# A hybrid decoder block on one core: the forms of the output products land in their places, two sets in turn on ScalarE's queue, with a third weight buffer and loads issued behind weight loads

## The chip, the cores and the metric

The program runs on one core of a Trainium2 chip. A core has TensorE (PE, matmuls), VectorE (DVE), ScalarE (ACT), GpSimd (POOL) and SyncE (SP), which work through instruction lists of their own and wait for one another by semaphores, and 16 DMA engines that move data between the chip's memory and the core's own memory. A transfer is issued by an instruction on one engine's list and then runs by itself; the engine waits at that instruction until what the transfer needs is there. The metric is device time in microseconds of one execution, the median of several runs; lower is better.

## The reference, cut to what matters

One decoder layer over 1024 tokens and 16 meta tokens, width 1024: half a SwiGLU step, a mixing step (a gated DeltaNet beside RWKV-7), half a SwiGLU step, a norm. The change lies in the two SwiGLU steps, and there in the second product.

```python
def _swiglu(x, w_gu, w_down):
    gate, up = jnp.split(x @ w_gu, 2, axis=-1)
    return (jax.nn.silu(gate) * up) @ w_down

h = h + 0.5 * _swiglu(_rmsnorm(h, ffn1_norm[l]), ffn1_w_gu[l], ffn1_w_down[l])
u = _rmsnorm(h, mix_norm[l])
...
h = h + merged @ w_out[l]
h = h + 0.5 * _swiglu(_rmsnorm(h, ffn2_norm[l]), ffn2_w_gu[l], ffn2_w_down[l])
return _rmsnorm(h, final_norm)[:, N_META:]
```

All of it is float32; w_gu is 1024 x 5632 and w_down 2816 x 1024.

## The kernel before, in words

**Precision.** A float32 matmul is made of three in the reduced type fp32r: `split` (lines 164 and 165) writes the high part of a tile on ScalarE (a copy, rounded) and the low part on VectorE (source minus high part); then high x high, high x low and low x high are added up in one accumulator. Every weight and every operand passes through such a pair of instructions.

**The two SwiGLU steps.** Each is a "gate_up" stage and a "down" stage, named gate_up1 and down1 for the first, gate_up2 and down2 for the second. Both stages use a product of 2 x 2 blocks by seven block products instead of eight. For down, tokens are cut into halves (columns of the transposed activations, n = 520 in the first step, 512 in the second) and the 2816 inner rows into two halves of 11 tiles of 128. The seven operands made of the activations' blocks are called **forms** (`FORMS`: b11, t1, t2, b22, t3, b21, t4); each has 11 tiles of 128 x n float32, 260 or 256 KB a tile. gate_up makes them unit by unit and stores them to memory (`frm`), on SP's list. In its last unit b11 is formed first, and t4 last.

**down** (from line 647) has seven rounds, r0 to r6, one for each form. A round runs over four m (128 output rows), and over two weight chunks of each m, of 6 and 5 inner tiles (128 x 768 and 128 x 640, 384 and 320 KB). For each chunk it multiplies 6 or 5 tiles, 3 times, for both column halves of n (in ffn2, n = 512 is one piece). So a round of down1 has 264 matmuls (line 667), one of down2 132 of twice the width. After each m the sum is added to up to four residual tiles (`h`, `hh`, line 673, VectorE): 4 of them in r0, then 2, 3, 1, 2, 1, 1. In down1 the rounds r5 and r6 are run twice, for columns 256 on and for the first 256, so that the norm of the next step can begin early; there each weight chunk is fetched twice and used for half as many matmuls.

**Weights.** `fetchw` takes a raw tile (`wraw`, two buffers), loads it on SP's list (line 233), splits it into a tile `w` (two buffers) and keeps one chunk ahead of the use (`AHEAD` = 1). In r0, r5 and r6 the raw tile is split itself. In r1 to r4 the weight is a sum or difference of blocks: POOL adds or subtracts the raw tile and a standing tile `wsum` (lines 239 to 246), and r1 and r4 load a second block into `wsum` first (lines 238, 245).

**Forms before.** `Hidden.load` loads a form tile into one of three staging tiles `hr` on SP's list (line 623). `Hidden.fill` splits it into a slot of a ring of 28 (tiles `fa`, `fb` in ffn1; `hdb`, `fs` in ffn2), as many tiles ahead of the round as slots allow. The residual tiles are loaded on POOL's list, all at the head of down (lines 735 and 834).

**What sets the order.** The builder emits instructions through a scheduling layer, so an engine's list is not the order of the code; the rows quoted with the change are from the built programs. Each engine's list is worked in order.

Of the kernel before, what the change touches and what calls it, by code (L numbers as in the profile page):

```python
# [227 lines left out]
def down_weights(g, name, raw, r, m, k0, kk):  # L228
# [4 lines left out]
    dma(raw, blk(*((0, 0), (1, 1), (0, 0), (0, 1), (1, 0), (0, 1), (1, 1))[r]))  # L233
    if r in (0, LAST, LAST + 1):
        return raw
    s = g.wsum[:, m, k0 : k0 + kk]
    if r == 1:
        dma(s, blk(1, 0))
        sums(s, s, raw, op=ALU.add)
    elif r == 2:  # L240
        sums(s, s, raw, op=ALU.subtract)
    elif r == 3:
        sums(s, raw, s, op=ALU.subtract)
    else:
        dma(s, blk(0, 0))
        sums(s, s, raw, op=ALU.subtract)
# [3 lines left out]
def fetchw(g):  # L250
# [10 lines left out]
    w = g.wp.tile([P, 2, KD, P], F32R, name="w", tag="w", bufs=WB)  # L261
# [4 lines left out]
def loadw(g, name, *idx):  # L266

    while g.wfetched < min(g.wused + 1 + AHEAD, len(g.worder)) and g.worder[g.wfetched]:
# [341 lines left out]
class Hidden:  # L610

    AHEAD = 3

    def __init__(self, g, pool, n):
        self.g, self.pool, self.n, self.raws, self.loaded = g, pool, n, [], 0
        self.order = [(r, p) for r in range(len(FORMS)) for p in range(HF)]
        self.slots, self.at = [], {}

    def load(self):
        r, p = self.order[self.loaded]  # L620
        self.loaded += 1
        raw = self.pool.tile([P, ROW(self.n)], F32, name="hr", tag="hr", bufs=self.AHEAD)[:, : self.n]
        self.g.nc.sync.dma_start(raw, self.g.frm[r, p][:, : self.n])
        self.raws.append(raw)

    def ahead(self):
        for _ in range(self.AHEAD):
            self.load()
        yield
        yield  # L630
        fetchw(self.g)
        yield
        yield
# [12 lines left out]


def slot_tile(pool, n, name):
    return pool.tile([P, 2, ROW(n)], F32R, name=name, tag=name, bufs=1)[:, :, :n]


def down(g, hs, which, n, hidden, hooks):

    nc = g.nc
    hidden.fill(HF + 5)
    for r, cols in down_rounds(which == 1):
        hidden.fill(HF * (r + 1))
        for m in range(HK):
            pd = mm_tile(g, "pd", n)
# [15 lines left out]
            if r <= LAST:  # L675
                hidden.fill(HF * r + 16 + 3 * (m + 1))
# [1143 lines left out]
```

## Time and profile before

| | us |
|---|---|
| median of 3 runs | 3102.53 (3102.46 to 3102.97) |
| the profiled execution | 3106.87 |
| its span, first to last instruction | 3105.1 |
| gate_up1's last products to the end of down1's matmuls | 468.65 to about 770 |
| gate_up2's last unit to the end of down2's matmuls | about 2811 to 3090 |
| TensorE busy over the span | 2928.2 (94%) |
| VectorE, ScalarE, POOL busy | 2192.1 (71%), 1456.7 (47%), 493.1 (16%) |
| mean granted TensorE clock | 0.981 |

The page's chain of waits gives the share of the span by the engine and line that the end waited for. The windows view gives, for each stretch of time, the busy time of every engine with its instructions in brackets, then the granted clock, the DMA engines' busy share and the rate in GB/s. A timeline row is a start, a length, engine, line and operation, and in square brackets the idle time before it and what ended that. Busy shares of the whole span say little here: down1 and down2 are some 18% of it and have limits of their own. A few matmul records can be missing, so counts differ by some from 264.

### The profile page before, as it was taken

What the parts mean: (1) busy time and instruction counts of PE and PEld (TensorE: products, weight loads), DVE (VectorE), ACT (ScalarE), POOL (GpSimd) and SP (SyncE); (2) the same over time, 40 slices, a digit from 0 to 9 for tenths busy, and PEclk for the clock granted to TensorE, in tenths of its full rate; (3) what the DMA queues carried; (4) which work ended last, traced back from release to release, by engine and by line L of the source; (5) the groups of instructions that cost most, each with busy time, mean ns of one, the idle gap of its engine ahead of it and who ended that gap; (6) DMA issues with size and microseconds to landing.
All of it is one profiled execution on the core that took longest, in us unless ns stands there. A gap on an engine that the chain in (4) does not pass through costs nothing.

```text
span 3105.1 us, 63103 instructions
## 1 busy us (share of the span) xinstructions
PE 2928.2 (94%) x25630; PEld 2519.8 (81%) x25630; DVE 2192.1 (71%) x4103; ACT 1456.7 (47%) x2562; POOL 493.1 (16%) x574
## 2 busy tenths in 40 slices
PE   8999997998989999999998999999999999998897
PEld 8999997887978888888776777777786888886676
DVE  7566666755677777877877888777766766666874
ACT  5222223334655565665566556665644432223343
POOL 0333321511010000000000100000000032331520
PEclk9999998999999999999999999999999999999999
DMA  3333237656223223332332332223345233336753
GB/s 124 98 103 103 103 132 243 211 149 174 90 66 77 62 70 82 79 84 73 100 93 71 78 83 79 77 73 84 109 146 177 75 106 102 102 102 224 237 174 111
DMA packets 294467, 351.52 MB, mean 113 GB/s; under 512 B 173392, under 2 KB 179536, under 8 KB 294176
## 3 DMA queue, kind: packets, MB, share of 16 engines
q1 hardware_dynamic: 289936, 335.68, 36.1%
q0 software_dynamic: 2512, 8.65, 0.8%
q8 instruction: 201, 3.29, 0.5%
q10 hardware_dynamic: 1728, 3.16, 0.3%
q14 instruction: 90, 0.74, 0.1%
HBM read 279.50 MB, written 67.91 MB: 112 GB/s over the span
## 4 chain that ended last, share of the span: by engine, by line
PE 66%; DVE 15%; DMA 8%; ACT 7%; issue 3%; SPq 0%; POOL 0%; DVEq 0%; ACTq 0%; POOLq 0%
PE pg L486 24%; PE pp L299 18%; PE pd L667 5%; DMA hr<-frm 4%; DVE w L165 3%; PE pg L510 3%; PE pwo L299 3%; ACT w L164 2%; DMA wraw<-in_wdn 2%; DVE tb L1482 1%; DVE Xb L1484 1%; PE vp L1167 1%; PE cs L1114 1%; PE mp L1167 1%; PE bkt L1399 1%
## 5 line engine op out<-in xcount | busy, mean ns | idle before, releaser
L299 PE MATMUL pp<-uk,w 128*128 128x512 f32 (+2 forms) x4824 | 969.3, 346 | 11.1 <-DVE w L165 6.0
L299 PEld LDWEIGHTS pp<-uk,w 128*128 128x128 f32 x4824 | 743.1, 190 | 107.9 <-DVE w L165 13.4
L165 DVE TENSOR_TENSOR w<-wraw,w 128x1024 fp32r<-128x1024 f32 (+2 forms) x314 | 393.8, 1255 | 112.4 <-ACT w L164 105.2
L164 ACT ACTIVATE w<-wraw 128x1024 fp32r<-128x1024 f32 (+2 forms) x314 | 314.4, 1002 | 284.6 <-PE pg L486 130.4
L486 PE MATMUL pg<-bt,w 128*128 128x256 f32 (+2 forms) x2520 | 404.2, 319 | 7.4 <-ACT w L164 6.7
L486 PEld LDWEIGHTS pg<-bt,w 128*128 128x128 f32 x2520 | 362.1, 189 | 42.2 <-ACT w L164 7.2
L492 DVE TENSOR_TENSOR c<-c,pg 128x520 f32<-128x520 f32 (+1 forms) x280 | 189.5, 689 | 245.8 <-PE pg L486 222.4
L486 PE MATMUL pg<-b,w 128*128 128x256 f32 (+2 forms) x2160 | 347.8, 317 | 0.0
L486 PEld LDWEIGHTS pg<-b,w 128*128 128x128 f32 x2160 | 309.7, 188 | 28.1
L667 PE MATMUL pd<-fa,w 128*128 128x256 f32 (+1 forms) x1200 | 173.5, 299 | 40.5 <-DVE w L165 19.1
L667 PEld LDWEIGHTS pd<-fa,w 128*128 128x128 f32 x1200 | 159.7, 201 | 51.1 <-DVE w L165 24.7
L164 ACT ACTIVATE w<-wrx 128x1024 fp32r<-128x1024 f32 (+1 forms) x64 | 58.4, 912 | 290.9 <-PE pg L486 247.7
L667 PE MATMUL pd<-fs,w 128*128 128x512 f32 x636 | 155.8, 401 | 14.0 <-ACT w L164 7.6
L456 POOL TENSOR_TENSOR wrx<-wrx 128x512 f32<-128x512 f32 x38 | 52.9, 1392 | 726.2 <-DVE w22b L165 547.2
L667 PEld LDWEIGHTS pd<-fs,w 128*128 128x128 f32 x636 | 122.0, 194 | 45.4 <-ACT w L164 9.8
L1484 DVE TENSOR_TENSOR Xb<-Xb,tb 115x126 f32<-115x126 f32 (+22 forms) x496 | 125.3, 253 | 8.8
L1482 DVE TENSOR_TENSOR tb<-Ub,Xb 115x126 f32<-115x126 f32 (+22 forms) x496 | 124.0, 250 | 8.3 <-DMA Ub<-scr 1.0
L1291 DVE SCALAR_TENSOR_TENSOR acc<-xr,pk,acc 128x528 f32<-128x528 f32 (+1 forms) x144 | 108.7, 756 | 29.1 <-ACT acc L1287 28.2
L299 PE MATMUL pwo<-uk,w 128*128 128x512 f32 x384 | 99.9, 413 | 4.1 <-DVE w L165 1.9
L165 DVE TENSOR_TENSOR w<-wsum,w 128x768 fp32r<-128x768 f32 x64 | 75.0, 1173 | 24.5 <-ACT w L164 24.1
L299 PEld LDWEIGHTS pwo<-uk,w 128*128 128x128 f32 x384 | 73.9, 197 | 21.9 <-ACT w L164 2.6
L164 ACT ACTIVATE w<-wsum 128x768 fp32r<-128x768 f32 x64 | 50.2, 785 | 83.5 <-PE pd L667 67.0
(441 smaller groups left out, 4940.4 us busy)
## 6 DMA issues: line engine op xcount, KB each, us to landing
wraw<-in_win SPq DMA_DIRECT2D x150, 512.0 KB
wraw<-in_wdn SPq DMA_DIRECT2D x64, 384.0 KB
wraw<-in_wgu SPq DMA_DIRECT2D x44, 512.0 KB
wrx<-in_wgu SPq DMA_DIRECT2D x44, 512.0 KB
wraw<-in_wdn SPq DMA_DIRECT2D x64, 320.0 KB
frm<-c SPq DMA_DIRECT2D x77, 260.0 KB
hr<-frm SPq DMA_DIRECT2D x77, 260.0 KB
frm<-c SPq DMA_DIRECT2D x77, 256.0 KB
```

The source lines that it names most:

```text
L164: g.nc.scalar.activation(hi, src, AF.Copy)
L165: (eng or g.nc.vector).tensor_tensor(lo, src, hi.bitcast(F32), op=ALU.subtract)
L299: g.nc.tensor.matmul(ps, lhsT=l, rhs=r, start=i == 0, stop=i == n - 1)
L456: sums.tensor_tensor(a22, a21, a22, op=ALU.add)
L486: nc.tensor.matmul(ps[:, c0 : c0 + cn], lhsT=l[:, x, k, :], rhs=r[:, k, y, c0 : c0 + cn], start=i == 0, stop=i == 3 * HK - 1)
L492: nc.vector.tensor_tensor(o, x, y, op=ALU.add)
L510: nc.tensor.matmul(ps[:, c0 : c0 + cn], lhsT=l[:, x, k, :], rhs=r[:, k, y, c0 : c0 + cn], start=i == 0, stop=i == 6 * HK - 1)
L667: nc.tensor.matmul(pd[:, c0 : c0 + cn], lhsT=wd[:, u, k - k0, :], rhs=x[:, v, c0 : c0 + cn], start=k + i == 0, stop=k == HF - 1 and i == 2)
L1167: g.nc.tensor.matmul(ps[e][HS[dst], c0 : c0 + CB], lhsT=l, rhs=r, start=True, stop=True)
L1291: nc.vector.scalar_tensor_tensor(acc[:, :n], xr[:, tap : tap + n], V("convw", ct * 4 + tap), acc[:, :n], op0=ALU.mult, op1=ALU.add)
L1482: nc.vector.tensor_tensor(tv, U[:, i, i + 1 :].unsqueeze(2).to_broadcast([npt, nt, ncc]), X[:, i, 0:ncc].unsqueeze(1).to_broadcast([npt, n ...
L1484: nc.vector.tensor_tensor(X[:, i + 1 :, 0:ncc], X[:, i + 1 :, 0:ncc], tv, op=ALU.add)
```

## The change

**Where forms lie.** There are no staging tiles any more. A form tile is loaded by DMA into the low half of its slot, `t[:, 1]`, on ScalarE's list (line 670), and is then split in place: the high part into `t[:, 0]`, the low part over the raw data. The slots are the operand tiles of gate_up (b11, b21, t2: the "even" set; t3, b22, t4, t1: the "odd" set) as gate_up's products release them. Round 0 uses the even set, round 1 the odd one, and so on in turn. Eight tiles of round 0 are loaded behind gate_up's last product with b11 and b21, three behind the last with t2, and all are split among gate_up's last units (`Hidden.ahead`). The forms of round r+1 are loaded and split at m = 1 to 3 of round r (`Hidden.step`).

**Weights.** In down every third chunk goes to a third split buffer, `w3`, and `loadw` fetches two chunks ahead instead of one. The raw tiles stay two.

**Loads behind weight loads.** The second blocks of r1 and r4, a load of constants (`ck`) and the residual tiles are issued on SP's list, each behind the weight load that was fetched last (`issue_after`); the residual tiles in round 0, two (in ffn2 four) transfers per m, and no longer on POOL's list.

TensorE's list has the same 19879 entries in the same kinds, VectorE's the same 4105. ScalarE's gains 154 DMA issues, SP's loses 130, POOL's 24.

ScalarE's list at the passage from gate_up1 to down1 (`c` are gate_up's values, `w` with a number, `wrx` and `w22b` weight tiles; a count at a row's end means that many rows in a row alike). Before:

```order
204 L499 ACTIVATE c_4706<-pg 128x520
205 L164 ACTIVATE w<-wraw 128x768
206 L164 ACTIVATE w<-wrx 128x1024
207 L601 ACTIVATE c_4802<-c_4802 128x520
208 L164 ACTIVATE w_133<-wraw 128x1024
209 L601 ACTIVATE c_4488<-c_4488 128x520
210 L601 ACTIVATE c_4750<-c_4750 128x520
211 L758 ACT_TABLE_LOAD
212 L164 ACTIVATE w<-wraw 128x640
213 L164 ACTIVATE fa_5049<-hr 128x520
214 L164 ACTIVATE fa_5050<-hr 128x520
```

With the change:

```order
204 L513 ACTIVATE c_4709<-pg 128x520
205 L670 DMA form<-frm 128x520 x8
206 L164 ACTIVATE w<-wraw 128x768
207 L164 ACTIVATE form<-form 128x520 x8
208 L164 ACTIVATE w<-wrx 128x1024
...
213 L798 ACT_TABLE_LOAD
214 L670 DMA form<-frm 128x520 x3
215 L164 ACTIVATE w_5084<-wraw 128x768
216 L164 ACTIVATE form<-form 128x520 x3
217 L670 DMA form<-frm 128x520 x2
218 L164 ACTIVATE w<-wraw 128x640
```

Eight loads and eight splits of forms moved ahead of two weight splits of gate_up's last unit (rows 208 and on), and the loads of the rest follow among down's weight splits.

SP's list at the same passage, from gate_up1's last stores (`frm<-c`) on. Before, and with the change:

```order
131 L516 DMA frm<-c_4706 128x520
132 L752 DMA ck<-in_ck 128x1200
133 L516 DMA frm<-c_4898 128x520
134 L516 DMA frm<-c_4750 128x520
135 L238 DMA wsum<-in_wdn 128x768
136 L238 DMA wsum<-in_wdn 128x640
137 L623 DMA hr<-frm 128x520 x3
138 L238 DMA wsum<-in_wdn 128x768
139 L238 DMA wsum<-in_wdn 128x640
140 L623 DMA hr<-frm 128x520 x3
```
```order
131 L233 DMA wraw<-in_wdn 128x640
132 L780 DMA h_5065<-in_hT 128x1040
...
137 L780 DMA h_5069<-in_hT 128x1040
138 L233 DMA wraw<-in_wdn 128x768
139 L233 DMA wraw<-in_wdn 128x640
140 L780 DMA h_5062<-in_hT 128x1040
141 L780 DMA h_5063<-in_hT 128x1040
142 L233 DMA wraw<-in_wdn 128x768
143 L240 DMA wsum<-in_wdn 128x768
144 L233 DMA wraw<-in_wdn 128x640
```

The loads of forms left SP's list and the residual tiles came in; six of these stand ahead of round 0's last two weight chunks (rows 138, 139). The second blocks moved from the head of the stage to behind the weight load with which each is summed.

The diff, cut to its core:

```diff
@@ down_weights
-    dma(raw, blk(*((0, 0), (1, 1), (0, 0), (0, 1), (1, 0), (0, 1), (1, 1))[r]))
+    g.wdma = dma(raw, blk(*((0, 0), (1, 1), (0, 0), (0, 1), (1, 0), (0, 1), (1, 1))[r]))
...
+    def other(i, j):
+        with g.tc.issue_after(g.wdma.ins):
+            dma(s, blk(i, j))
+
     if r == 1:
-        dma(s, blk(1, 0))
+        other(1, 0)
         sums(s, s, raw, op=ALU.add)
...
     else:
-        dma(s, blk(0, 0))
+        other(0, 0)
         sums(s, s, raw, op=ALU.subtract)
@@ fetchw, loadw
-    w = g.wp.tile([P, 2, KD, P], F32R, name="w", tag="w", bufs=WB)
+    third = False
+    if name.startswith("wdn"):
+        g.wcount += 1
+        third = g.wcount % 3 == 0
+    if third:
+        w = g.wthird.tile([P, 2, CHUNKS[0][1], P], F32R, name="w3", tag="w3", bufs=1)
+    else:
+        w = g.wp.tile([P, 2, KD, P], F32R, name="w", tag="w", bufs=WB)
...
-    while g.wfetched < min(g.wused + 1 + AHEAD, len(g.worder)) and g.worder[g.wfetched]:
+    while g.wfetched < len(g.worder) and g.worder[g.wfetched]:
+        if g.wfetched > g.wused + AHEAD + g.worder[g.wfetched][0].startswith("wdn"):
+            break
         fetchw(g)
@@ class Hidden
-    AHEAD = 3
...
-        raw = self.pool.tile([P, ROW(self.n)], F32, name="hr", tag="hr", bufs=self.AHEAD)[:, : self.n]
-        self.g.nc.sync.dma_start(raw, self.g.frm[r, p][:, : self.n])
...
     def ahead(self):
-        for _ in range(self.AHEAD):
-            self.load()
+        self.g.wcount = 0
+        self.even += self.places("11", "21")
+        self.slots = self.even[:]
+        self.load(8, 0)
         yield
         yield
         fetchw(self.g)
+        self.split(3)
         yield
+        self.even += self.places("t2")
+        self.slots = self.even[:HF]
+        self.load(HF, 0)
+        self.split(6)
         yield
+        self.split(8)
         yield
         fetchw(self.g)
+        self.split(HF)
         yield
...
+    def arrange(self, spare, last):
+        e, o = self.even, self.odd
+        self.slots = e[:HF] + (o[:HF] + e[:HF]) * 2 + o[HF:] + [spare] + o[:HF] + last
+
+    def load(self, upto, done):
+        while len(self.loads) < min(upto, len(self.slots)):
+            i = len(self.loads)
+            rp, t = self.order[i], self.slots[i]
+            if max([-9] + [r for (r, _), o in self.loads if o is t]) >= done:
+                break
+            self.g.nc.scalar.dma_start(t[:, 1, :].bitcast(F32), self.g.frm[rp][:, : self.n])
+            self.loads.append((rp, t))
+
+    def split(self, upto):
         while len(self.at) < min(upto, len(self.order)):
...
+            rp, t = self.loads[len(self.at)]
+            split(self.g, t[:, 1, :].bitcast(F32), t[:, 0, :], t[:, 1, :])
             self.at[rp] = t
...
+    def step(self, r, m):
+        self.load(HF * (r + 1) + ((0, 4, 8, 11) if r else (3, 6, 9, 11))[m], r - (m == 0))
+        self.split(HF * (r + 1) + (0, 0, 4, 8)[m])
@@ down
-    hidden.fill(HF + 5)
     for r, cols in down_rounds(which == 1):
-        hidden.fill(HF * (r + 1))
         for m in range(HK):
+            hidden.step(r, m)
+            if r == 0:
+                hooks.residual(m)
...
-            if r <= LAST:
-                hidden.fill(HF * r + 16 + 3 * (m + 1))
@@ ffn1 (ffn2 likewise, two transfers a tile)
-        for k in pairs:
-            nc.gpsimd.dma_start(hs[k], g.a["hT"][k])
...
+        def residual(m):
+            for k in (m, m + HK):
+                with tc.issue_after(g.wdma.ins):
+                    nc.sync.dma_start(hs[k], g.a["hT"][k])
```

93 lines of the change are left out of this document (46 added, 47 removed).

## The prediction

> **What bounds the kernel now.** I read the page first, for the chain of waits and the cost of the output products ("down", line 667), then the windows view cut at the rounds of both down stages, then the timeline where a round is longest. The page:
>
> ```profile
> span 3105.1 us, 63103 instructions
> PE 66%; DVE 15%; DMA 8%; ACT 7%; issue 3%; SPq 0%; POOL 0%; DVEq 0%; ACTq 0%; POOLq 0%
> PE pg L486 24%; PE pp L299 18%; PE pd L667 5%; DMA hr<-frm 4%; DVE w L165 3%; PE pg L510 3%; PE pwo L299 3%; ACT w L164 2%; DMA wraw<-in_wdn 2%; DVE tb L1482 1%; DVE Xb L1484 1%; PE vp L1167 1%; PE cs L1114 1%; PE mp L1167 1%; PE bkt L1399 1%
> ```
>
> TensorE carries the chain, but the loads of forms (hr<-frm) have 4% of the span, and down itself only 5%: it is waited for, not bound by its own matmuls. The pace that down could have stands in the last products of the two gate_up stages, 24 matmuls of half width and 12 of full width back to back:
>
> ```profile
> 468.65 3.03 PE L486 MATMUL pg<-b,w 128*128 128x256 f32 x24
> 471.51 3.03 PE L486 MATMUL pg<-bt,w22b 128*128 128x256 f32 x24
> ...
> 477.96 2.08 PE L667 MATMUL pd<-fa,w 128*128 128x256 f32 x8 [3.31 <-DVE fa L165]
> 486.77 0.58 PE L667 MATMUL pd<-fa,w 128*128 128x256 f32 x1 [6.73 <-ACT fa L164]
> ...
> 489.01 14.81 PE L667 MATMUL pd<-fa,w 128*128 128x256 f32 x91 [0.15 <-DVE fa L165]
> ```
>
> From 468.65 to 471.51 is 2.86 us for 24, or 0.119 us each; after the 6.73 us stall 91 take 14.81, or 0.163 each. A round of down1 is 4 m x 11 k x 3 products x 2 halves = 264 matmuls: 31.6 us at the first pace. What the seven rounds took (the last two, run by halves, together):
>
> ```profile
> core 0: us, PE busy (x) PEld busy (x) DVE busy (x) ACT busy (x) POOL busy (x), PEclk, DMA share, GB/s
> 474.30:531.30 57.00, 40.49 (x268) 37.55 (x267) 34.94 (x52) 20.77 (x32) 5.10 (x5) 0.82 0.82 277
> 531.30:568.70 37.40, 33.59 (x265) 32.98 (x264) 32.23 (x33) 14.62 (x22) 23.93 (x13) 0.95 0.73 222
> 568.70:604.90 36.20, 32.41 (x264) 31.59 (x263) 25.35 (x31) 12.60 (x19) 17.47 (x10) 1.00 0.62 190
> 604.90:644.10 39.20, 34.75 (x268) 34.07 (x267) 25.06 (x25) 12.59 (x19) 14.51 (x8) 0.91 0.63 199
> 644.10:678.10 34.00, 32.11 (x265) 31.56 (x264) 19.16 (x26) 12.58 (x19) 0.71 (x1) 1.00 0.38 116
> 678.10:770.30 92.20, 77.06 (x538) 69.65 (x536) 54.52 (x76) 40.16 (x61) 8.85 (x6) 0.96 0.63 172
> ```
>
> Seven rounds could take 221 us and take 296: 75 us are lost, 25 of them in round 0, where the granted clock fell to 0.82. That cold clock is the second loss behind a stall; the Trainium skill ("TensorE: Matmul & The Clock Gate", Part 1) says that a window of some 3.4 us without work halves the clock, and the 0.163 us behind the 6.73 us stall agrees. Now down2, 132 matmuls of full width a round:
>
> ```profile
> 2816.02 2.88 PE L486 MATMUL pg<-bt,w 128*128 128x512 f32 x12
> 2825.65 1.22 PE L486 MATMUL pg<-bt,w 128*128 128x512 f32 x2 [6.75 <-ACT w L164]
> ...
> 2837.77 2.88 PE L486 MATMUL pg<-b,w 128*128 128x512 f32 x12
> 2840.49 2.88 PE L486 MATMUL pg<-bt,w22b 128*128 128x512 f32 x12
> ```
> ```profile
> 2843.20:2885.10 41.90, 34.39 (x133) 26.55 (x132) 29.49 (x42) 15.97 (x25) 8.42 (x11) 0.92 0.89 301
> 2885.10:2917.70 32.60, 30.47 (x133) 24.39 (x132) 29.06 (x31) 13.43 (x21) 20.43 (x11) 1.00 0.76 240
> ...
> 2917.70:2956.30 38.60, 33.66 (x134) 26.63 (x133) 30.67 (x34) 15.31 (x23) 22.57 (x12) 0.91 0.66 202
> 2956.30:2988.50 32.20, 30.63 (x131) 24.05 (x130) 24.71 (x25) 12.01 (x18) 12.47 (x7) 1.00 0.77 251
> 2988.50:3021.10 32.60, 31.14 (x134) 24.51 (x133) 19.55 (x28) 15.75 (x25) 2.83 (x2) 1.00 0.39 123
> 3021.10:3058.90 37.80, 33.59 (x136) 25.93 (x135) 21.62 (x28) 16.25 (x23) 2.96 (x2) 0.95 0.43 132
> ```
>
> 12 in 2.72 us is 0.227 each, a round 29.9 us; the first six took 215.7 where 179.4 would do, and the seventh runs at its pace. Ahead of it gate_up2 stands still for 6.75 us.
>
> **Which wait ends last.** For forms, and for ScalarE at two of the stalls:
>
> ```profile
>   DMA hr<-frm: 80.8, 40
> ...
> 486.08 0.64 ACT L164 ACTIVATE fa<-hr 128x520 fp32r<-128x520 f32 x1 [14.87 <-DMA hr<-frm]
> ...
> 2820.17 0.63 ACT L164 ACTIVATE hdb<-hr 128x512 fp32r<-128x512 f32 x1 [8.02 <-DMA hr<-frm]
> ```
>
> The first line is of the tile hr over down1: its splits wait 80.8 us, 40 times, for the load into the staging tile. At 486.08 and 2820.17 ScalarE, which works in order, has stood on one such split for 14.87 and 8.02 us, and the split of the weight that TensorE needs stands behind it.
>
> **The change part by part.** *Round 0's forms.* Now eight of eleven are loaded and split while gate_up's last units run, the last three behind t2's last product. What then still costs in round 0 is VectorE: 8 weight splits, 11 form splits, 16 residual additions.
>
> ```profile
> L165 DVE TENSOR_TENSOR fa<-hr,fa 128x520 fp32r<-128x520 f32 x50 | 44.5, 916 | 32.1 <-ACT fa L164 32.0
> L673 DVE SCALAR_TENSOR_TENSOR h<-pd,h 128x520 f32<-128x520 f32 x48 | 31.1, 691 | 14.7 <-PE pd L667 14.6
> L165 DVE TENSOR_TENSOR w<-wraw,w 128x768 fp32r<-128x768 f32 x19 | 18.2, 957 | 26.6 <-ACT w L164 26.5
> L165 DVE TENSOR_TENSOR w<-wraw,w 128x640 fp32r<-128x640 f32 x19 | 15.6, 822 | 3.8 <-ACT w L164 3.8
> ```
>
> 4 x (0.957 + 0.822) + 11 x 0.916 + 16 x 0.691 = 7.1 + 10.1 + 11.1 = 28.3 of 31.6 us, nearly full: between 31.6 and, if the additions hold up weight splits as often as the old splits did, some 40. The transfers give a second bound: residuals 4.3, weights 2.9 and round 1's forms 2.9 MB at the 277 to 301 GB/s of the two first rounds are 34 to 36 us. I take 35.5, so 57.0 to 35.5 is **-21.5**. In down2 the same sum leaves 1.6 of 29.9 us; I take 34.5, so 41.9 to 34.5 is **-7.4**.
>
> *Rounds 1 to 4 of down1, 1 to 5 of down2.* The forms of round r+1 now go to slots that died a round before, at m = 1 to 3, so no split waits for a staging tile. With the third buffer a weight is split two chunks before its use: one m of a round is 66 matmuls or 7.9 us for two chunks, so the lead grows from about 4 us to about 8. Over the whole of down1 TensorE waited for weight splits and form splits like this (engine waited for, us, times):
>
> ```profile
>   DVE w L165: 54.5, 62
>   ACT w L164: 24.7, 30
> ...
>   ACT fa L164: 14.0, 3
>   DVE fa L165: 8.6, 8
> ```
>
> Down1: 37.4, 36.2, 39.2, 34.0 = 146.8 become 33, 33, 33, 34 = 133, **-13.8**; full pace, the upper bound, would give 20.4, and I leave 5 us for weights that POOL sums late. Round 4 (and 1) keep their time apart: their second block is now issued behind the weight load that it goes with, not a round ahead, so a pair must land and be summed on POOL within the two raw buffers' turn. Down2: 32.6 + 38.6 + 32.2 + 32.6 + 37.8 = 173.8 become 31.5 + 31.5 + 31.2 + 31.5 + 32.3 = 158, **-15.8**, between nothing and the 24.3 that full pace would give.
>
> *Rounds 5 and 6 of down1, by halves.* Here the matmuls per chunk halve and the raw weight bounds:
>
> ```profile
> 721.39 0.85 ACT L164 ACTIVATE w<-wraw 128x768 fp32r<-128x768 f32 x1 [1.95 <-DMA wraw<-in_wdn]
> 722.27 0.96 DVE L165 TENSOR_TENSOR w<-wraw,w 128x768 fp32r<-128x768 f32 x1 [1.97 <-ACT w L164]
> ...
> 727.00 0.85 ACT L164 ACTIVATE w<-wraw 128x768 fp32r<-128x768 f32 x1 [0.25 <-DMA wraw<-in_wdn]
> ```
>
> A 768 chunk of weights comes each 5.61 us (721.39 to 727.00), while the 33 matmuls that one m has there need 33 x 0.119 = 3.95 us. The cycle is the load, then 0.85 on ScalarE, then 0.96 on VectorE, which frees the raw tile for the next load. The raw tiles stay two, so the third split buffer does not shorten it: 16 turns of it are 89.8 of the 92.2 us. I take off the rest, 2.4, and part of one chunk's lead at the start, 1.3: **-3.7**; bounds 0 and the whole gap to pace, 92.2 - 63.2 = 29.
>
> *The tail of gate_up2.* The residual loads, 16 on POOL's queue around 2811, held the forms up; they now go on SP's queue behind weight loads, in round 0. The 8.02 us wait and its 6.75 us of idle TensorE go, except for form splits that now stand ahead of the unit's weights: 8 loads after b11's last product, 8 splits of 0.64, a few us of slack by my count: **-7**, bounds -8.5 (with the slow matmuls behind it) and 0. Gate_up1 has no such stall to lose, and could gain one in the same way: I take 0 there, with up to 5 lost.
>
> *Issues.* 154 DMA issues join ScalarE's queue. Its busy time in a round is 12.6 to 20.8 of over 34 us; 11 issues more at the nearest row,
>
> ```profile
> L735 POOL DMA_DIRECT2D h<-in_hT x3 | 1.6, 528 | 29.4 <-DMA wraw<-in_wdn 21.0 <-DMA frm<-c 8.4
> ```
>
> 0.53 us on POOL, are at most 5.8 us, so they hide unless an issue must itself wait. The Trainium skill ("DMA: Bandwidth & Descriptors", "Issuing engines are not separate DMA queues") says that another engine's queue saves issue time alone, since the same 16 engines carry all; by that rule the loads land no sooner for being on ScalarE, and the gain is from starting earlier, which the sum assumes anyway.
>
> Sum: -21.5 - 7.4 - 13.8 - 15.8 - 3.7 - 7.0 = **-69**. The profiled run took 3106.9 us, 4.3 above the median of 3102.5: 3106.9 - 69 = 3037.7, and as a median about **3034**.
>
> **Rivals.** *A: the third buffer also lifts rounds 5 and 6.* If two loads in flight plus a third split buffer let the queue run ahead, the 5.61 us cycle shrinks toward 3.95: 20 us more, 3014. Against it: the raw tile is freed only by VectorE's split.
>
> *B, slower: ScalarE's queue blocks.* An issue there waits until its slot is free (TensorE's last read) and until older transfers on the semaphore it shares with SP's loads have landed; behind it stand the weight splits. From 77 loads per stage, 11 in a round: if each holds ScalarE 1.8 us (260 KB at the 172 to 277 GB/s of the rounds take 0.9 to 1.5, and waits add), that is 20 us on top of 14 to 18 of work, more than the 31.6 us round: 34 to 38, so each round is 2 to 6 us late, and with matmuls at the 0.163 us of the cold clock for some 50 of them another 2: about 8 at the worse end, for 12 rounds +96. Against the 69 that leaves +27, 3130. It decides from about 1.3 us a load. For it: no load stands on ScalarE's queue in these stages before. Against: the order puts the loads early, when the slots have been dead for half a round.
>
> *C: VectorE and the transfers bind instead.* VectorE is busy 34.9, 32.2 and 29.5 us in the first rounds; SP now sends 3.2 MB of residuals ahead of round 0's last weights, and rounds 1 and 4 load two blocks per chunk in turn. If half the stalls only move there, -35: 3068.
>
> **How the numbers follow.** Forecast 0.53, A 0.12, B 0.13, C 0.22. The range 3006 to 3082 takes in A with some 8 us to spare and C with 14, and leaves out B and the 0.06 between C and B that I count as no change (0.03 from each). A measurement of this kernel tells about 0.2%, 6 us, from no change: faster 0.84, same 0.06, slower 0.10.
>
> **What would show it.** Round 0 of down1 near 35 us with a clock over 0.95; no split waiting for a form by more than a few us; waits of TensorE on weight splits under a third of the 79 us in down1; TensorE idle under 2 us ahead of down2; rounds 5 and 6 still with a weight each 5.4 to 5.6 us. It is wrong if ScalarE shows waits on its DMA issues ahead of weight splits (B), if VectorE is over 95% busy in rounds 0 to 2 while TensorE waits for it (C), or if rounds 5 and 6 fall under 75 us (A).

## The result, and the profile after

| | before | with the change |
|---|---|---|
| median, us | 3102.49 (3099.89 to 3102.97, 4 runs) | 3061.11 (3059.19 to 3063.64, 4 runs) |
| ratio to before | | 0.9869, interval 0.9852 to 0.9886 |
| profiled execution and its span | 3106.87, 3105.1 | 3060.95, 3058.4 |
| mean granted clock | 0.981 | 0.986 |

The change makes the kernel 41 us faster. 3034 us was forecast, a gain of 69 us: the direction holds and the time is in the range, but two fifths of the gain are missing. The profile page of the changed kernel, its chain of waits and the group of down's matmuls:

```profile
span 3058.4 us, 62929 instructions
PE 48%; DVE 10%; ACT 6%; DMA 3%; issue 2%; POOL 1%; SPq 0%; ACTq 0%; DVEq 0%; POOLq 0%
L700 PE MATMUL pd<-form,w 128*128 128x256 f32 (+2 forms) x2652 | 444.7, 328 | 43.4 <-DVE w L165 22.3
```

DMA fell from 8% of the chain to 3%, and loads of forms no longer lead it. The profiled execution of the kernel before lies 4 us above its median, so the spans differ by 46.7 us. Where these went is read from the rounds. The windows view of the changed kernel, cut near the ends of the first five rounds of down1, then 5 and 6 together, then the first three of down2 (same columns as before the change; the count behind TensorE's busy time, set against 264 or 132, tells how far a cut lies off the round's end):

```profile
474.10:512.30 38.20, 33.32 (x258) 32.82 (x257) 26.39 (x40) 14.40 (x23) 3.41 (x2) 0.91 0.93 329
512.30:549.40 37.10, 33.97 (x267) 33.38 (x266) 27.84 (x31) 12.21 (x20) 20.07 (x11) 0.95 0.74 249
549.40:589.30 39.90, 35.40 (x268) 34.69 (x267) 26.54 (x31) 12.06 (x19) 20.26 (x12) 0.91 0.59 179
589.30:622.00 32.70, 32.70 (x276) 32.70 (x275) 21.36 (x25) 12.04 (x19) 13.95 (x6) 1.00 0.66 223
622.00:654.30 32.30, 30.84 (x254) 30.40 (x254) 22.92 (x32) 15.16 (x24) 3.83 (x2) 1.00 0.58 180
654.30:742.00 87.70, 74.89 (x542) 69.53 (x540) 54.10 (x72) 38.36 (x57) 10.39 (x8) 0.96 0.64 179
```
```profile
2805.20:2839.80 34.60, 31.22 (x133) 24.27 (x131) 25.16 (x40) 13.20 (x22) 1.61 (x1) 1.00 1.01 363
2839.80:2881.10 41.30, 33.55 (x128) 25.89 (x129) 32.97 (x31) 13.64 (x21) 25.64 (x14) 0.92 0.75 244
2881.10:2914.60 33.50, 31.64 (x131) 25.21 (x130) 28.84 (x30) 11.85 (x19) 19.46 (x10) 0.95 0.60 187
```

The later sections compare many kernels by rounds. The table counts down's matmuls from the first on, 264 or 132 to a round, in each profiled execution; all 1848 and 924 of them are in every trace. A round runs from the start of its first matmul to the start of the next round's first, so a wait just ahead of a round counts to the one before it. Each row is one execution:

| run | down1 r0 | r1 | r2 | r3 | r4 | r5+r6 | down2 r0 | r1 | r2 | r3 | r4 | r5 | r6 |
|---|---|---|---|---|---|---|---|---|---|---|---|---|---|
| before | 56.9 | 37.6 | 36.4 | 39.1 | 34.2 | 91.3 | 42.0 | 33.9 | 37.6 | 32.7 | 32.5 | 38.3 | 30.1 |
| change | 39.2 | 37.0 | 39.7 | 31.6 | 33.7 | 86.6 | 35.8 | 41.2 | 34.1 | 29.9 | 34.1 | 33.2 | 30.1 |
| e1 two split buffers | 41.8 | 41.6 | 39.2 | 32.8 | 39.2 | 89.1 | 36.4 | 42.4 | 36.4 | 33.2 | 32.5 | 37.9 | 30.1 |
| e2 second blocks early | 42.7 | 37.0 | 40.3 | 31.6 | 33.9 | 87.4 | 40.3 | 35.1 | 40.3 | 29.9 | 33.7 | 32.9 | 30.1 |
| e3 forms on POOL's list | 34.6 | 36.2 | 49.1 | 32.0 | 38.9 | 87.1 | 41.8 | 34.2 | 43.6 | 33.3 | 32.0 | 33.7 | 30.1 |
| e4 raw tile late | 39.0 | 37.4 | 40.4 | 31.6 | 35.1 | 71.7 | 36.2 | 43.0 | 33.0 | 29.9 | 33.6 | 32.9 | 30.1 |
| e5 no second blocks | 37.1 | 33.7 | 36.4 | 31.6 | 31.6 | 86.1 | 34.1 | 31.0 | 42.1 | 29.9 | 29.9 | 32.9 | 30.1 |
| e6 no sums | 38.9 | 31.6 | 31.6 | 31.6 | 31.6 | 87.4 | 34.5 | 29.9 | 29.9 | 29.9 | 30.4 | 32.2 | 30.1 |
| e7 sums on VectorE | 38.6 | 31.6 | 39.4 | 36.6 | 31.6 | 87.3 | 34.4 | 33.2 | 29.9 | 33.6 | 31.4 | 32.9 | 30.1 |
| e8 forms on SP's list | 31.6 | 32.9 | 38.6 | 35.8 | 34.4 | 89.1 | 30.7 | 31.1 | 40.8 | 29.9 | 32.7 | 33.0 | 30.1 |
| e9 SP, VectorE, raw tile | 31.6 | 31.6 | 31.6 | 31.6 | 31.6 | 71.5 | 29.9 | 32.0 | 29.9 | 29.9 | 29.9 | 33.1 | 30.1 |
| e10 e9, POOL in r3 and r4 | 31.6 | 31.6 | 31.6 | 41.1 | 40.4 | 73.2 | 29.9 | 32.0 | 29.9 | 40.1 | 35.1 | 33.3 | 30.1 |
| e11 before, sums on VectorE | 55.4 | 31.8 | 34.6 | 32.4 | 33.2 | 90.4 | 38.6 | 34.8 | 30.7 | 31.5 | 31.7 | 38.5 | 30.1 |
| e12 VectorE, raw tile | 36.6 | 32.0 | 38.8 | 35.5 | 31.8 | 72.0 | 34.6 | 34.0 | 29.9 | 34.0 | 30.2 | 32.9 | 30.1 |

So the span's 46.7 us are: down1's round 0, 17.7; rounds 1 to 4, 5.3 (147.3 to 142.0); rounds 5 and 6, 4.7; what lies from down1's end to down2's start, 10.1 (2073.4 to 2063.3); down2's round 0, 6.2; its rounds 1 to 5, 2.5 (175.0 to 172.5); the rest small. Of gate_up2's stall nothing is left, TensorE's timeline runs through from gate_up2 to down2:

```profile
2788.85 11.06 PE L500 MATMUL pg<-bt,w 128*128 128x512 f32 x48
...
2802.46 2.88 PE L500 MATMUL pg<-bt,w22b 128*128 128x512 f32 x12
2805.18 7.19 PE L700 MATMUL pd<-form,w 128*128 128x512 f32 x31
```

The missing gain lies in rounds 1 to 5: 7.8 us came where 29.6 were forecast. Round 3 does reach TensorE's pace in both stages, but round 2 of down1 and round 1 of down2 became longer, by 3.3 and 7.3 us. Three stalls of the changed kernel, one of them in round 0, show what holds TensorE up. The timeline of down1's round 0 (a DMA row on a list that ends in q is the issue, its length the time from the first of the run of issues to the end of the last, waits included):

```profile
484.32 10.31 SPq L780 DMA_DIRECT2D h<-in_hT  x6
...
489.28 3.07 ACTq L670 DMA_DIRECT2D form<-frm  x2
492.40 0.64 ACT L164 ACTIVATE form<-form 128x520 fp32r<-128x520 f32 x1 [3.28 <-DMA form<-frm]
...
494.72 1.61 SPq L233 DMA_DIRECT2D wraw<-in_wdn  x2
...
501.77 1.57 ACT L164 ACTIVATE w<-wraw 128x768 fp32r<-128x768 f32 x2 [0.29 <-DMA wraw<-in_wdn]
502.67 0.79 PE L700 MATMUL pd<-form,w 128*128 128x256 f32 x2 [4.68 <-ACT w L164]
```

Two issues take ScalarE 3.07 us, and six splits of forms stand before the weight split for which TensorE waits 4.68 us. In the built program these six are forms of round 5: their slots are free, and the scheduling layer moved their loads forward. The weight split itself waits last for its own load (0.29 us). That load was issued at 494.72, behind six residual loads on SP's list and after the loads of these six forms, and landed at 501.67; from 494.7 to 501.7 the DMA engines had a share of 1.04 and moved 415 GB/s. So here early loads made a weight late, more than the list did. In round 2 it is the issues alone:

```profile
553.41 8.01 ACTq L670 DMA_DIRECT2D form<-frm  x4
561.54 0.84 ACT L164 ACTIVATE w<-wsum 128x768 fp32r<-128x768 f32 x1 [12.28 <-POOL wsum L248]
562.44 0.79 PE L700 MATMUL pd<-form,w 128*128 128x256 f32 x2 [4.05 <-ACT w L164]
```

Four loads hold ScalarE's list for 8 us, and the weight split behind them starts 0.1 us after the last. The view names a sum on POOL (L248) as its releaser; that sum belongs to the next round, so the list was what it waited for. These issues wait on semaphores that they share with SP's weight loads, which themselves wait for a raw tile: the longest wait, 4.9 us up to an issue at 560.61, is in the trace's events for the semaphore of a weight load issued at 557.03. And in round 1 of down2, at a stall of TensorE for a weight whose high part ScalarE had written by 2862.75, VectorE and POOL:

```profile
2859.52 5.49 DVE L165 TENSOR_TENSOR form<-form 128x512 fp32r<-128x512 f32 x4
2859.75 2.13 POOL L244 TENSOR_TENSOR wsum<-wsum,wraw 128x768 f32<-128x768 f32 x1 [0.97 <-DMA wsum<-in_wdn]
...
2865.67 4.32 DVE L165 TENSOR_TENSOR form<-form 128x512 fp32r<-128x512 f32 x2
2869.91 1.28 DVE L706 SCALAR_TENSOR_TENSOR hh<-pd,hh 128x512 f32<-128x512 f32 x2
2871.11 3.09 DVE L165 TENSOR_TENSOR w<-wsum,w 128x768 fp32r<-128x768 f32 x2
...
2873.52 16.74 PE L700 MATMUL pd<-form,w 128*128 128x512 f32 x66 [4.01 <-DVE w L165]
```

The first four form splits take 5.49 us: two of them run alone and take 0.68 each, two run beside a sum on POOL and take 2.31 and 2.05. The next two, both beside sums, take 4.32; the weight's low part stands behind them all, and itself takes 2.36 beside a sum.

### The profile page after: what moved, and what is told of

It reads as the page before. It is cut to its first block, busy times and chain, and to the rows that moved or that the text cites. A ratio compares the mean times of both kernels' runs of the same rounds, so it can differ in the third digit from the quotient of the medians.

```text
span 3058.4 us, 62929 instructions
## 1 busy us (share of the span) xinstructions
PE 2909.5 (95%) x25630; PEld 2510.0 (82%) x25630; DVE 2181.6 (71%) x4103; ACT 1448.8 (47%) x2562; POOL 481.8 (16%) x550
## 3 DMA queue, kind: packets, MB, share of 16 engines
q1 hardware_dynamic: 271216, 303.44, 33.1%
## 4 chain that ended last, share of the span: by engine, by line
PE 48%; DVE 10%; ACT 6%; DMA 3%; issue 2%; POOL 1%; SPq 0%; ACTq 0%; DVEq 0%; POOLq 0%
PE pp L313 16%; PE pg L500 12%; PE pd L700 3%; PE pwo L313 3%; DVE w L165 2%; ACT w L164 1%; PE pg L524 1%; DVE tb L1524 1%; DVE Xb L1526 1%; PE cs L1156 1%; PE vp L1209 1%; DMA wsum<-in_wdn 1%; PE mp L1209 1%; DMA wraw<-in_wdn 1%; DVE mt L1632 1%
## 5 line engine op out<-in xcount | busy, mean ns | idle before, releaser
L313 PEld LDWEIGHTS pp<-uk,w 128*128 128x128 f32 x4824 | 741.5, 190 | 110.2 <-DVE w L165 15.8
L700 PE MATMUL pd<-form,w 128*128 128x256 f32 (+2 forms) x2652 | 444.7, 328 | 43.4 <-DVE w L165 22.3
L700 PEld LDWEIGHTS pd<-form,w 128*128 128x128 f32 x2652 | 393.3, 194 | 93.9 <-DVE w L165 32.3
L1333 DVE SCALAR_TENSOR_TENSOR acc<-xr,pk,acc 128x528 f32<-128x528 f32 (+1 forms) x144 | 108.8, 756 | 28.9 <-ACT acc L1329 28.3
L165 DVE TENSOR_TENSOR form<-form 128x512 fp32r<-128x512 f32 (+1 forms) x149 | 123.1, 871 | 7.5 <-ACT form L164 7.5
L164 ACT ACTIVATE form<-form 128x512 fp32r<-128x512 f32 (+1 forms) x149 | 84.6, 623 | 42.5 <-DMA form<-frm 31.6
```

The costliest lines, as they stand in the source:

```text
L164: g.nc.scalar.activation(hi, src, AF.Copy)
L165: (eng or g.nc.vector).tensor_tensor(lo, src, hi.bitcast(F32), op=ALU.subtract)
L313: g.nc.tensor.matmul(ps, lhsT=l, rhs=r, start=i == 0, stop=i == n - 1)
L700: nc.tensor.matmul(pd[:, c0 : c0 + cn], lhsT=wd[:, u, k - k0, :], rhs=x[:, v, c0 : c0 + cn], start=k + i == 0, stop=k == HF - 1 and i == 2)
L1333: nc.vector.scalar_tensor_tensor(acc[:, :n], xr[:, tap : tap + n], V("convw", ct * 4 + tap), acc[:, :n], op0=ALU.mult, op1=ALU.add)
```

## The experiments

All but e11 start from the changed kernel (3061.1 us). The runs come from several chips, on which the kernel before took 3099.4 to 3102.5 us (medians), so a difference between kernels of different chips is good to about 3 us.

**e1: the third buffer undone.**

```diff
-        third = g.wcount % 3 == 0
+        third = False
...
-        if g.wfetched > g.wused + AHEAD + g.worder[g.wfetched][0].startswith("wdn"):
+        if g.wfetched > g.wused + AHEAD:
```

> The change without its third split-weight buffer: two buffers, one chunk fetched ahead, all else as changed (3061.1 us). Theory 1 (the third buffer bought what the rounds 1 to 4 gained): 15 to 25 us lost, 3076 to 3086, TensorE's waits on weight splits over both down stages back over 130 us from 101 (32.3 + 27.5 + 13.4 + 28.2). Rival (the gain is all from forms that start early and the waits left are of loads, which a deeper queue of splits cannot shorten): under 6 us lost, 3061 to 3067.

3083.1 us (3076.6 to 3086.1), 22 us lost, and TensorE's waits on weight splits are 144 us (51.4 and 35.4 in down1, 47.9 and 9.4 in down2). Theory 1 holds: the third buffer carries half of the change's gain, most of it in rounds 1 and 4 of down1 and in down2. Without it, rounds 1 and 4 of down1 take longer than in the kernel before (41.6 and 39.2 against 37.6 and 34.2). So they did gain from it, and something else took it back.

**e2: the second blocks early.**

```diff
     if r == 1:
-        other(1, 0)
         sums(s, s, raw, op=ALU.add)
...
+def second(g, name, r, m):
+
+    i = 1 if r == 1 else 0
+    for k0, kk in CHUNKS:
+        with g.tc.issue_after(g.wdma.ins):
+            g.nc.sync.dma_start(g.wsum[:, m, k0 : k0 + kk], g.a[name][m + HK * i][:, k0 : k0 + kk])
...
+SECOND = {(0, 1): ((1, 0),), (0, 2): ((1, 1),), (0, 3): ((1, 2), (1, 3)),
+          (3, 0): ((4, 0),), (3, 1): ((4, 1),), (3, 2): ((4, 2),), (3, 3): ((4, 3),)}
...
                 wd = loadw(g, f"wdn{which}", r, m, k0)
+                if k0:
+                    for q in SECOND.get((r, m), ()):
+                        second(g, f"wdn{which}", q[0], q[1])
```

> The second blocks of rounds 1 and 4 are issued one to three m ahead (in round 0 from its second m on, in round 3 behind each m), not each behind the weight load that it is summed with. Theory (round 1 is bound by the pair load, second load, POOL's sum within the turn of two raw tiles): round 1 falls from 37.0 to about 33 us in down1 and from 41.4 to about 34 in down2, with round 0, whose transfers already fill 93 to 100%, longer by up to 4 each; in all -3 to -11 us, 3050 to 3058. Rival (round 1 waits for VectorE beside POOL's sums): round 1 stays within 2 us of 37.0 and 41.4, time 3059 to 3066.

3068.0 us (3061.8 to 3074.0), beyond both ranges. Round 1 of down1 stays at 37.0; that of down2 falls from 41.2 to 35.1, near the 34 of the theory, but its rounds 0 and 2 become longer by 4.5 and 6.2, and round 0 of down1 by 3.5. So the pair of loads does hold up round 1 of down2 and not that of down1, and moving it early costs more than it gives.

**e3: the loads of forms on POOL's list.**

```diff
-            self.g.nc.scalar.dma_start(t[:, 1, :].bitcast(F32), self.g.frm[rp][:, : self.n])
+            self.g.nc.gpsimd.dma_start(t[:, 1, :].bitcast(F32), self.g.frm[rp][:, : self.n])
```

> The loads of forms go on POOL's list instead of ScalarE's, nothing else moved. Theory (in round 2 ScalarE stands at its own load issues, which wait for older loads of SP on shared semaphores, and the weight split stands behind them): the 4.05 us stall of TensorE at the start of round 2 goes, with the cold clock after it 5 to 7 us in down1's round 2 (39.9 to about 34), and as much in part of down2; but POOL's sums now stand behind loads, so rounds 1 to 4 can lose what is won: 3050 to 3062. Rival (ScalarE's issues cost nothing): no round falls by over 1 us; 3061 to 3075, slower by POOL's longer issue.

3090.8 us (3087.3 to 3092.0), slower than both ranges. Down1's rounds 0 and 1 become faster (34.6 and 36.2), round 2 takes 49.1: the loads now stand behind the sums on POOL's list, and the forms come late. The waits view of that kernel around round 2 (engine and line, what it waited for, us, times, longest), and of its timeline, POOL's list there:

```profile
ACT form L164 <- DMA form<-frm: 20.1, 5, 16.1
...
PE pd L700 <- ACT w L164: 9.5, 1, 9.5
```
```profile
553.98 3.34 POOL L246 TENSOR_TENSOR wsum<-wsum,wraw 128x768 f32<-128x768 f32 x2 [1.75 <-DMA wraw<-in_wdn]
557.26 4.26 POOL L670 DMA_DIRECT2D form<-frm  x8
```

The first issue comes at 557.26, behind the last sums of round 2; ScalarE stands 16.1 us at a form split, and the weight split behind it keeps TensorE waiting 9.5. Off ScalarE round 0 of down1 is 4.6 us shorter, so the place of the loads there costs; but on another busy list they come too late themselves.

**e4: a third raw tile in the rounds by halves.** In rounds 5 and 6 of down1 (`halved`) the third buffer serves as a raw tile, and one chunk is fetched ahead in place of two.

```diff
+    late = halved(name, idx)
+    if late and g.wcount % 3 == 2:
+        raw = g.wthird.tile([P, 2, CHUNKS[0][1], P], F32R, name="w3", tag="w3", bufs=1)[:, 0, :kk].bitcast(F32)
+    else:
+        raw = g.wp.tile([P, KD, P], F32, name="wraw", tag="wraw", bufs=2)[:, :kk]
...
-        third = g.wcount % 3 == 0
+        third = g.wcount % 3 == 0 and not late
...
-        if g.wfetched > g.wused + AHEAD + g.worder[g.wfetched][0].startswith("wdn"):
+        nxt = g.worder[g.wfetched]
+        if g.wfetched > g.wused + AHEAD + (nxt[0].startswith("wdn") and not halved(*nxt[:2])):
```

> In the rounds by halves of down1 (5 and 6) the third buffer serves as a third raw tile instead of a third split tile, all else as changed. Theory (these rounds turn on load, high part, low part within two raw tiles, 5.6 us a turn): a third raw tile brings them from 86.4 to 68 to 74 us, so 3045 to 3050. Rival (TensorE there waits for the splits themselves or for bandwidth): 84 to 90 us, time 3058 to 3066.

3050.3 us (3046.2 to 3052.7), 10.8 faster, and the two rounds fall by 14.9, from 86.6 to 71.7. The splits of 768 chunks on ScalarE's timeline, first in the changed kernel, then in e4:

```profile
671.25 0.84 ACT L164 ACTIVATE w<-wraw 128x768 fp32r<-128x768 f32 x1 [0.29 <-DMA wraw<-in_wdn]
676.77 0.84 ACT L164 ACTIVATE w<-wraw 128x768 fp32r<-128x768 f32 x1 [1.56 <-DMA wraw<-in_wdn]
```
```profile
676.93 0.85 ACT L164 ACTIVATE w<-w 128x768 fp32r<-128x768 f32 x1 [1.08 <-PE pd L709]
681.11 0.85 ACT L164 ACTIVATE w<-wraw 128x768 fp32r<-128x768 f32 x1 [1.13 <-PE pd L709]
```

5.52 us from one to the next becomes 4.18, and the split now waits for TensorE and not for the load. That the raw tile's turn bounds these rounds is shown.

**e5 and e6: without second blocks, and without sums.**

```diff
     if r == 1:
-        other(1, 0)
-        sums(s, s, raw, op=ALU.add)
+        sums(s, raw, raw, op=ALU.add)
...
-        other(0, 0)
-        sums(s, s, raw, op=ALU.subtract)
+        sums(s, raw, raw, op=ALU.subtract)
```
```diff
-    if r in (0, LAST, LAST + 1):
+    if True:
         return raw
```

> Leaves out a part of the computation: the second blocks of rounds 1 and 4 are not loaded, and POOL sums the raw tile with itself in their place, so POOL's and VectorE's work is as before and 2.9 MB a round fewer move. Theory (round 1 waits for VectorE, whose splits take 1.4 to 1.5 us beside POOL's sums and 0.7 to 1.0 alone): round 1 stays at 36 to 38 us in down1 and 38 to 41 in down2, VectorE's form splits still near 1.5 us there. Rival (the pair of loads): round 1 at 32 to 34 and 31 to 34.

> Leaves out a part of the computation: rounds 1 to 4 use the raw weight tile itself, with no second block and no sum on POOL. Theory (POOL's sums slow VectorE down): VectorE's form splits near 0.7 us in every round, round 1 at 32 to 34 us in down1 and 30 to 33 in down2, rounds 1 to 4 of down1 together 130 to 135 from 143, and of down2 126 to 132 from 139. Rival (what is left in these rounds comes from ScalarE's blocked list or late loads): rounds 1 to 4 within 4 us of 143 and 139.

Both leave out a part of the computation. One run each: 3042.6 and 3021.6 us. Without second blocks, round 1 falls to 33.7 and 31.0, as the rival had it for down2, but round 2 of down2 rises to 42.1: there TensorE waits 4.9 us for weight splits behind form issues (three of them take 7.11 us of ScalarE's list) and then for VectorE beside POOL. Without sums, rounds 1 to 4 of down1 take 126.4 (from 142.0), those of down2 120.1 (from 139.3), and a form split takes 0.7 us in each. The rival of e6 falls: POOL's sums, with what they wait for and delay, are nearly all that holds these rounds up.

**e7: the sums on VectorE.**

```diff
-    sums = g.nc.gpsimd.tensor_tensor
+    sums = g.nc.vector.tensor_tensor
```

> The sums of weight blocks in rounds 1 to 4 are made on VectorE instead of POOL. Theory (a sum on POOL costs VectorE more than it takes off it: 11 form splits 0.8 us longer each and 8 weight splits 0.4, some 10 us in down2's round 1, against 8 sums of about 0.9 us, 7 us): 3050 to 3063, form splits back at 0.7 us, round 1 at 34 to 37 us in down1 and 34 to 38 in down2. Rival (POOL's help is worth what it costs): slower, 3066 to 3090, with VectorE over 95% busy in rounds 1 and 2.

3045.5 us (3044.6 to 3045.9), 15.6 faster. VectorE's groups by line from 2838 to 2876 us, most of it down2's round 1, of the changed kernel and of e7:

```profile
L165 DVE TENSOR_TENSOR form<-form 128x512 fp32r<-128x512 f32 x11 | 16.0, 1503 | 0.0
L165 DVE TENSOR_TENSOR w<-wsum,w 128x768 fp32r<-128x768 f32 x5 | 7.2, 1448 | 6.4 <-ACT w L164 6.4
...
L706 DVE SCALAR_TENSOR_TENSOR hh<-pd,hh 128x512 f32<-128x512 f32 x10 | 6.4, 678 | 0.0
```
```profile
L165 DVE TENSOR_TENSOR form<-form 128x512 fp32r<-128x512 f32 x11 | 7.3, 689 | 0.0
L165 DVE TENSOR_TENSOR w<-wsum,w 128x768 fp32r<-128x768 f32 x6 | 5.7, 953 | 0.0
```

In the mean a form split takes 1.50 us in the kernel in which POOL sums and 0.69 in the other, a weight split 1.45 and 0.95; the residual addition, which reads the accumulator, takes 0.68 in both. VectorE does more instructions in less time. Another thing changes with this word: a sum of 128 x 768 itself takes 0.96 us on VectorE and 1.80 or more on POOL, and these runs don't part the two gains. Down1's rounds 2 and 3 stay long (39.4, 36.6): there ScalarE's list still stands, with four issues that take 8.29 us at 579.59.

**e8: the loads of forms on SP's list.**

```diff
-            self.g.nc.scalar.dma_start(t[:, 1, :].bitcast(F32), self.g.frm[rp][:, : self.n])
+            self.g.nc.sync.dma_start(t[:, 1, :].bitcast(F32), self.g.frm[rp][:, : self.n])
```

> The loads of forms go on SP's list instead of ScalarE's, as ever behind the weight loads that the builder orders ahead of them. Theory (ScalarE's list is blocked by its own load issues): TensorE's waits on ScalarE's weight splits (32.3 us in down1, 13.4 in down2) fall to under half, rounds 0 and 2 of down1 to 34 to 36 us from 38.4 and 38.8; 3048 to 3057. Rival (a list that mixes forms with weights makes the weights late, as in the kernel before): rounds 1 to 4 longer by 1 to 3 us each, 3063 to 3085.

3043.2 us (3041.6 to 3050.4), 17.9 faster (13.6 by the ratios to the kernel before on each chip). The first three rounds of down1 in the windows view of e8:

```profile
474.00:505.50 31.50, 31.50 (x266) 31.50 (x264) 21.62 (x34) 10.02 (x15) 2.61 (x2) 1.00 0.93 336
505.50:538.40 32.90, 31.94 (x266) 31.63 (x265) 29.54 (x31) 14.51 (x24) 18.45 (x11) 1.00 0.86 290
538.40:577.00 38.60, 33.02 (x267) 32.00 (x266) 37.47 (x35) 13.66 (x21) 25.21 (x13) 1.00 0.66 201
```

Round 0 runs at TensorE's pace, 31.5 us, with the DMA engines as busy (0.93) as in the changed kernel; the last two weight loads of the round are issued at 484.6 and 490.5 here, at 494.7 and 496.0 there. TensorE's waits on ScalarE's weight splits fall to 20.9 and 5.6 us, in down1 less than the theory had it, and round 2 does not gain as forecast: VectorE is busy 37.5 of its 38.6 us, with POOL 25.2 beside it. With the list free, that round is bound by VectorE.

**e9, e10 and e12: together.** e9 joins e4, e7 and e8; e10 has VectorE's sums in rounds 1 and 2 alone; e12 is e9 with the forms still on ScalarE's list. The one new line is e10's:

```diff
-    sums = g.nc.gpsimd.tensor_tensor
+    sums = (g.nc.vector if r < 3 else g.nc.gpsimd).tensor_tensor
```

> Three edits together on the changed kernel: forms loaded on SP's list, the sums of weight blocks on VectorE, and the third buffer as a raw tile in down1's rounds by halves. Theory (three separate losses: ScalarE's blocked list 18 us, VectorE beside POOL 16, the raw turn 11 by the medians of the single runs; the first two overlap in round 2): 3012 to 3026, round 2 at 32 to 34 us in down1 and 30 to 32 in down2, VectorE's form splits at 0.7. Rival (VectorE, with the sums on top, becomes the bound once the others are gone): 3028 to 3042, rounds 1 and 2 at 34 to 38 us.

> As the three edits together, but the sums are on VectorE in rounds 1 and 2 alone, where it has the residual additions of two or three tiles an m, and on POOL in rounds 3 and 4. Theory (a sum on POOL slows VectorE wherever both run; but round 3 has one addition an m and room for it): within 4 us of the run with all sums on VectorE, 3012 to 3030. Rival (VectorE's list is the bound in round 3 too): 5 to 12 us slower than that run.

> As the run of all three edits, but the forms' loads stay on ScalarE's list: sums on VectorE and the late raw tile alone. By adding the two single gains (15.6 and 10.8 from 3061.1) it is 3035, and the list of the forms' loads is then worth 33 us and not the 18 that it gave alone: theory, that both losses sit at the same places and each hides the other. Rival (the three edits gain more together through the raw tile or the sums): 3015 to 3025, so that the list is again worth about 18.

e9 takes 3001.4 us (3000.5 to 3002.5), 0.9684 of before (0.9671 to 0.9698), 60 us under the change: better than expected. Its windows over down1:

```profile
474.00:505.50 31.50, 31.50 (x266) 31.50 (x265) 24.30 (x37) 10.19 (x16) 0.00 (x0) 1.00 0.96 351
505.50:537.30 31.80, 31.80 (x268) 31.80 (x267) 30.98 (x45) 16.11 (x26) 0.00 (x0) 1.00 0.94 316
537.30:568.70 31.40, 31.40 (x265) 31.40 (x265) 29.92 (x44) 12.66 (x19) 0.00 (x0) 1.00 0.68 226
568.70:600.50 31.80, 31.80 (x269) 31.80 (x268) 24.63 (x35) 13.05 (x20) 0.00 (x0) 1.00 0.81 282
600.50:632.00 31.50, 31.50 (x266) 31.50 (x265) 19.97 (x29) 13.46 (x21) 0.00 (x0) 1.00 0.42 145
632.00:703.80 71.80, 67.77 (x534) 65.05 (x533) 54.18 (x73) 39.72 (x59) 10.91 (x8) 1.00 0.74 219
```

TensorE is busy in every microsecond of rounds 0 to 4, at full clock. VectorE, busy 31.0 of 31.8 us in round 1, doesn't hold it up: e9's rival falls. e12 takes 3031.1 us (3024.6 to 3032.3), 30.0 under the change, near the sum of 15.6 and 10.8. So the forms' list is worth 29.7 us behind the other two edits and 17.9 alone (28.5 and 13.6 by the ratios): the theory of e12 holds, the two losses sat in the same rounds and each hid part of the other. Round 2 of down1 takes 39.7 us in the changed kernel, 39.4 and 38.8 with the sums alone mended (e7, e12), 38.6 with the list alone (e8) and 31.6 with both (e9).

e10 takes 3034.5 us (3020.2 to 3039.8), 33 over e9, and its rounds 3 and 4 of down1 take 41.1 and 40.4. Its theory falls, and the size goes beyond its rival. The timeline of e10 ahead of round 3's longest stall:

```profile
573.09 6.34 SPq L679 DMA_DIRECT2D form<-frm  x11
577.43 0.64 ACT L164 ACTIVATE form<-form 128x520 fp32r<-128x520 f32 x1 [11.29 <-DMA form<-frm]
...
581.12 0.79 PE L709 MATMUL pd<-form,w 128*128 128x256 f32 x2 [4.61 <-ACT w L164]
```

Eleven loads stand together on SP's list, ScalarE waits 11.29 us at the first split, and the weight split stands behind it: the picture of the kernel before. Why the order came out so with sums on POOL in that round wasn't tried further.

**e11: the kernel before, with its sums on VectorE.** The edit is e7's.

> The kernel before with the sums of weight blocks on VectorE in place of POOL, nothing else. Theory (VectorE beside POOL was a loss before the change too, hidden behind the waits for forms): some 4 to 12 us faster than before, its splits at 0.7 and 0.8 to 0.96 us in rounds 1 to 4. Rival (before the change the forms' loads bound these rounds and VectorE's time is free): within 3 us of it.

3070.2 us (3068.5 to 3072.9) against 3099.4, ratio 0.9909 (0.9893 to 0.9925): 29 us, far over the expected 4 to 12. One group of VectorE's form splits (tiles `fa`) from 531 to 680 us, which holds rounds 1 to 4 of down1, of before and of e11:

```profile
L165 DVE TENSOR_TENSOR fa<-hr,fa 128x520 fp32r<-128x520 f32 x33 | 33.0, 1029 | 14.9 <-ACT fa L164 14.9
```
```profile
L165 DVE TENSOR_TENSOR fa<-hr,fa 128x520 fp32r<-128x520 f32 x33 | 22.5, 697 | 6.4 <-ACT fa L164 6.4
```

One word gives seven tenths of what the whole change gives. Round 0 of down1 (55.4) hardly moves. Not all of it is in the rounds with sums: gate_up2's last 96 matmuls take 25.1 us in place of 32.6, since the stall of 6.75 us is one of 1.70 here, and why is open.

## Why the prediction was right, and where it was not

**Round 0's forms: right in kind, 3.8 and 1.2 us short.** -17.7 and -6.2 came of -21.5 and -7.4. The reason given for stopping at 35.5 was VectorE at 28.3 of 31.6 us and transfers at 34 to 36. VectorE was busy 26.4 us of the 38.2 and was not what TensorE waited for. The transfers did hold the round up, but by their order and not by their sum: a weight landed late behind residuals and forms of round 5, while e8 runs this round in 31.5 us with the DMA engines at 336 GB/s.

**Rounds 1 to 5: the failed step.** "-13.8" and "-15.8" came as -5.3 and -2.5. That no split waits long for a staging tile any more is right (for its load a form split of down1 waits 3.3 us at most), and so is the larger lead (e1, 22 us). The step took the rest of TensorE's waits to be a matter of lead. Two things that the sum put at nothing here took most of the gain back (e9, with both mended, has these rounds at TensorE's pace but for round 1 and 5 of down2). First, VectorE's splits beside POOL's sums: the step leaves 5 us for weights that POOL sums late and has no term for VectorE, and round 0's sum took a form split at 0.916 us, the mean of a row. That mean was a mixture of 0.70 alone and 1.3 in the mean, up to 2.36, beside POOL. The Trainium skill ("SBUF — State Buffer", "Who interferes with whom") says that a VectorE instruction with two inputs in the core's own memory and a POOL instruction that reads it keep each other out. The trace agrees, by 1.503 against 0.689 us, and by the additions with an input in the accumulator, 0.68 in both; that rule spoke against this step and the prediction didn't weigh it.

Second, ScalarE's list, rival B's mechanism: it did not make the kernel slower, but it stands in round 2 of down1, at 8.01 us for four issues. B priced it at 1.8 us a load in every round; it is worth 14 to 30 us over the kernel (e8, e9 against e12), not 96: 33 of the 154 issues begin more than 1 us behind what stands ahead of them on the list.

**The issues, "they hide unless an issue must itself wait".** Some had to wait. The prediction drew on the rule of the Trainium skill ("DMA: Bandwidth & Descriptors", "Issuing engines are not separate DMA queues") that another engine's list saves issue time alone, and its sum put the choice of the list at nothing. By e9 and e12 it matters by some 30 us: through what stands behind an issue that waits, and in round 0 through the loads that land ahead of a weight.

**Second blocks just in time: a loss in one round.** Round 1 of down2 falls by 6.1 us when they come early (e2) and by 10.2 without them (e5), so there the pair of loads has a part; other rounds lose more than that, and the kernel as a whole gains nothing by e2.

**Rounds 5 and 6: right.** -4.7 of -3.7, a weight each 5.5 us, and the raw tile as the cause (e4). Rival A is out for the third split buffer; for a raw tile its 20 us were 14.9 in the rounds and 10.8 in the kernel's time.

**The tail of gate_up2: right in kind,** -10.1 of -7 and beyond its bound of -8.5, by the stall and the slow matmuls behind it (the last 96 matmuls take 21.8 us in place of 32.6). That the residual loads on POOL's list were the cause isn't shown: e11 leaves them there and loses most of the stall. Gate_up1 lost nothing.

Rival C named VectorE and the transfers, and 3068 was nearer to the time than the forecast; but it had VectorE short of time by its own work, and e9 gives it more work and the best time.

Of the signs, TensorE without a stall ahead of down2 and a weight each 5.5 us came; round 0 near 35 us at a clock over 0.95 (39.2, 0.91) and waits under a third of 79 us in down1 (59.8) didn't, and B's sign, waits at ScalarE's issues ahead of weight splits, did show. That the time lies in the range is in part luck: the range was wide enough to take in C. The prediction's 0.163 us for a matmul at the cold clock, which B's price uses, is a mean over two clocks: behind that stall a matmul took 0.22 us up to 495 us, at a granted clock of 0.50 to 0.54, and 0.12 us from there on.

## What to carry to other kernels

A group's mean that is far over its shortest instruction is a row to open before it is used as a price: what runs beside the long ones may be the cost, and e11 shows that an engine lent as help (POOL for sums) can cost more than it takes off, by its own longer instructions and by those that it holds up. A load belongs on a list whose next instructions can wait as long as the load's own semaphores may; two such faults in one round hide each other, so mending one of them shows too little.

## What the runs showed that was not expected

POOL's sum holds VectorE's two-input operations up: in the mean 0.69 to 1.50 us (form split) and 0.95 to 1.45 (weight split), and up to 2.3 for a single form split, while the accumulator's addition keeps its 0.68. DMA engines at a share of 0.93 to 0.96 and 336 to 351 GB/s did not delay TensorE in e8 and e9; the share alone told nothing of a bound. The e9 kernel, 3001.4 us, is the fastest here, 60 us under the change and 98 under before.
